# Tree attention: V's copies of the first 128 nodes move from GpSimd to VectorE, and loads and stores are reordered

## The chip, the cores and the metric

The kernel runs on one core of a Trainium2 chip. The metric is device time in microseconds (us) of one execution. The kernel before takes 140.92 us (median of three runs, 140.81 to 143.45). The profile read below spans 138.3 us from the first to the last instruction; the run that it belongs to was timed at 140.06 us, so a time contains about 2 us that the span does not.

## The reference

There are 8 batches of 12 heads, so 96 heads, each with 512 positions of 64 numbers. The positions are the nodes of a binary tree in heap order, and a node attends only to itself and to its ancestors:

```python
mask = np.zeros((seq, seq))
for i in range(seq):
    mask[i, i] = 1
    parent = i
    while parent > 0:
        parent = (parent - 1) // 2
        mask[i, parent] = 1
scores = np.einsum('bhqd,bhkd->bhqk', Q, K) * scale
scores = scores + (1 - mask) * (-1e9)
weights = np.exp(scores - np.max(scores, axis=-1, keepdims=True))
weights = weights / (np.sum(weights, axis=-1, keepdims=True) + 1e-10)
return np.einsum('bhqk,bhkd->bhqd', weights, V).astype(np.float32)
```

Q, K and V are float32 of 12.58 MB each, and so is the output.

## The kernel before, in words

**Units of work.** Heads are loaded by groups of eight (the code's `o`, here an *octet*; there are 12), computed by pairs (`i`, 48 iterations, four to an octet) and stored by groups of four (`q`, 24 stores of two iterations each). Position 4p+t of a head lies in partition p, slot t.

**Loads (lines 179 to 205).** Every load is a DMA that GpSimd issues, and each turns float32 into bfloat16 on the way, so 2 bytes are read from memory for each byte that lands. An octet takes six: K and Q (512 KB each as landed), V's partitions 64 to 127 (256 KB), V's partitions 32 to 63 straight into the value tile `vt` in two pieces (64 KB each, line 201), and V's partitions 0 to 31 (128 KB). The staging pools hold four octets. There are four value tiles.

**V's copies.** `values` needs V rows in the order of the key tiles. `spread_top` (line 207) copies V's partitions 0 to 31, the nodes under 128, into all four quarters of the value tile with four copies of 32 x 512 numbers; before the change they run on GpSimd (line 209). `spread_leaves` (line 221) and `spread_l7` (line 234) rearrange the rest on VectorE: three copies of 64 x 1024 numbers for an octet (lines 223 and 236). The first octet has forms of its own by four heads (line 245).

**One iteration.** TensorE does `scores1(i)` and `scores2(i)` (lines 292 to 329), then `values(i - 1)` (line 346), then `transpose(i + 2)` (line 259, K's part first, then Q's). ScalarE takes the exponentials of both score tiles (lines 307 and 331). VectorE does `norm(i - 1)`: a reciprocal (line 372) and a multiplication (line 375) that frees the only output tile `ob`; then `evac(i + 2)`, which copies the transposed K and Q out of PSUM (line 285) and frees the only transpose tile `kqp`; then what `spread_vector(i)` hands it. Every engine works in the order written.

**The order on GpSimd.** `pool_program` (line 394) is a list written by hand: loads of octet `o`, then `spread_top(o - 1)`, then two stores that lie `BEHIND` = 8 groups behind the loads, and so on for `o` = 2 to 11; at the end the remaining stores, with the last `spread_top` among them. In the compiled program each of GpSimd's DMAs waits for the landing of the eighth one before it, so at most eight are under way; an octet's six loads and two stores are eight. The last group of four heads is stored in pieces by the queues of SyncE and ScalarE.

**The order on VectorE.** `spread_vector(i)` (line 435) takes `divmod(i + 2, 4)`: at i = 4o - 2 the first leaf copy of octet o, at i = 4o - 1 the second one and `spread_l7`. `values` of octet o begins in iteration 4o + 1.

Of the kernel before, what the change touches and what calls it, by code (L numbers as in the profile page):

```python
# [107 lines left out]
def kernel(  # L108
# [7 lines left out]
    nc = tc.nc  # L116
# [4 lines left out]
    NQ = B * H // 4  # L121
# [57 lines left out]
    def load(kept, name, pool, src, o, h0=0, n=8, rows=(0, 128)):  # L179

        if o not in kept:
            kept[o] = pool.tile([P, 8, 4, D], bf16, name=name)
        nc.gpsimd.dma_start(  # L183
            out=kept[o][rows[0]:rows[1], h0:h0 + n, :, :].rearrange("p h t d -> p h (t d)"),
            in_=src[rows[0]:rows[1], 8 * o + h0:8 * o + h0 + n, :],
        )

    def load_k(o, h0=0, n=8):
        load(ksts, "kst", loads, Kr, o, h0, n)

    def load_q(o, h0=0, n=8):
        load(qsts, "qst", loads, Qr, o, h0, n)

    def load_v(o, *args):
        load(vsts, "vst", vloads, Vr, o, *args)

    def load_v_tiles(o):

        load_v(o, 0, 8, (64, 128))
        for half in range(2):  # L200
            nc.gpsimd.dma_start(  # L201
                out=vts[o % NV][32 * half:32 * half + 32, :, VCOL[1]:VCOL[1] + 2 * D],
                in_=Vr[32:64, 8 * o:8 * o + 8, 2 * D * half:2 * D * half + 2 * D],
            )
        load_v(o, 0, 8, (0, 32))

    def spread_top(o, h0=0, h1=8):
        for j in range(4):
            nc.gpsimd.tensor_copy(  # L209
                out=vts[o % NV][32 * j:32 * j + 32, h0:h1, VTOP:VTOP + D],  # L210
                in_=vsts[o][0:32, h0:h1, UNITS[TOP + j][1], :],
            )

    def tile_pair(o, p, h0, h1, first):

        c, step = VCOL[first], VCOL[first + 2] - VCOL[first]
        return vts[o % NV][p:p + 64, h0:h1, c:c + 2 * step].rearrange(
            "p h (t d) -> p h t d", t=2
        )[:, :, :, 0:D]

    def spread_leaves(o, upper, h0=0, h1=8):

        nc.vector.tensor_copy(  # L223
            out=tile_pair(o, 64 if upper else 0, h0, h1, upper),
            in_=vsts[o][64:128, h0:h1, upper:3 + upper:2, :],
        )
# [7 lines left out]
    def spread_l7(o):  # L234

        nc.vector.tensor_copy(  # L236
            out=tile_pair(o, 64, 0, 8, 0),
            in_=swapped(vts[o % NV][0:64, :, VCOL[3]:VCOL[3] + D], -D),
        )
# [142 lines left out]
    def store(eng, q, h0=0, n=4):  # L382
        eng.dma_start(  # L383
            out=Or[:, 4 * q + h0:4 * q + h0 + n, :],
            in_=ofs[q][:, h0:h0 + n, :, :].rearrange("p h t d -> p h (t d)"),
        )


    BEHIND = 8

    AHEAD = 3
    NO = NQ // 2

    def pool_program():

        for h0 in (0, 2):
            load_k(0, h0, 2)
            load_q(0, h0, 2)
        load_v(0, 0, 4)
        load_k(0, 4, 4)  # L400
        load_q(0, 4, 4)
        load_v(0, 4, 4)
        load_k(1, 0, 4)
        load_q(1, 0, 4)
        spread_top(0, 0, 4)
        load_v_tiles(1)
        load_k(1, 4, 4)
        load_q(1, 4, 4)
        spread_top(0, 4, 8)
        yield  # L410
        yield
        for o in range(2, NO):
            load_k(o)
            load_q(o)
            load_v_tiles(o)
            spread_top(o - 1)
            yield
            for q in (2 * o - BEHIND, 2 * o + 1 - BEHIND):
                if q >= 0:
                    store(nc.gpsimd, q)  # L420
        for q in range(NQ - BEHIND, NQ - 1):
            yield
            store(nc.gpsimd, q)
            if q == NQ - BEHIND + AHEAD:
                spread_top(NO - 1)

    def spread_first(quad, parts):

        for part in parts:
            if part < 4:  # L430
                spread_l7_natural(0, part, 4 * quad, 4 * quad + 4)
            else:
                spread_leaves(0, part - 4, 4 * quad, 4 * quad + 4)

    def spread_vector(i):

        if i == 1 or i == 2:
            spread_first(1, range(3) if i == 1 else range(3, 6))
        o, step = divmod(i + 2, 4)
        if 1 <= o < NO:  # L440
            if step == 0:
                spread_leaves(o, 0)
            elif step == 1:
                spread_leaves(o, 1)
                spread_l7(o)

    def pool_until(done, wanted):
        while done < wanted:
            next(program, None)
            done += 1  # L450
        return done

    program = pool_program()
    steps = pool_until(0, 1)
    transpose(0)
    evac(0)
    for i in range(NP + 1):
        if i < NP:
            scores1(i)
            scores2(i)  # L460
        if i == 1:
            transpose(2)
            evac(2)
            spread_first(0, range(4, 6))
        if i >= 1:
            values(i - 1)
            norm(i - 1)
        for n in (1 if i == 0 else i + 2,):
            if n < NP:
                transpose(n)  # L470
                evac(n)
        if i == 0:
            spread_first(0, range(4))
        spread_vector(i)
        if steps < NO:
            steps = pool_until(steps, min((i + 11) // 4, NO))
        else:
            steps = pool_until(steps, min(steps + 2, NO + (i - 2) // 2 - (NQ - 1 - BEHIND)))
        if i == NP - 1:
            store(nc.sync, NQ - 1, 0, 2)  # L480
# [32 lines left out]
```

The softmax here doesn't subtract the row's maximum and nothing guards it: scores larger than these inputs give would overflow.

## Time and profile before

| | before |
|---|---|
| time, median | 140.92 us |
| span of the profile | 138.3 us |
| granted TensorE clock, mean | 0.972 |
| busy: TensorE, VectorE, ScalarE, GpSimd | 107.7, 96.5, 84.3, 102.1 us |
| GpSimd's copies (line 209) | 52 copies, 31.1 us |
| first K landed, first exponential | 5.2 us, 8.05 us |
| exponential of iterations 7 and 47 starts | 30.48 us, 130.12 us |
| last multiplication of `norm` ends | 134.3 us |

The page of a profile gives busy times by engine, then the span in 40 slices of 3.46 us with the busy tenths of each engine, the share of the DMA engines and the rate at which bytes landed. The groups below it name a source line, an engine, an operation with its shapes, its count, its busy time, the mean of one in ns, and what ended the idle time before it. The waits say who sat idle until whom. The timeline lists instructions as start, duration, engine, line, operation, with the idle time ahead of it in square brackets. `L209` is line 209.

GpSimd's busy time counts the issuing of DMAs; a large one takes it 0.75 to 0.9 us. The landing rate counts bytes as they arrive in bfloat16, so a load of 197 GB/s reads 394 GB/s of memory.

### The profile page before, as it was taken

What the parts mean: (1) busy time and instruction counts of PE and PEld (TensorE: products, weight loads), DVE (VectorE), ACT (ScalarE), POOL (GpSimd) and SP (SyncE); (2) the same over time, 40 slices, a digit from 0 to 9 for tenths busy, and PEclk for the clock granted to TensorE, in tenths of its full rate; (3) what the DMA queues carried; (4) which work ended last, traced back from release to release, by engine and by line L of the source; (5) the groups of instructions that cost most, each with busy time, mean ns of one, the idle gap of its engine ahead of it and who ended that gap; (6) DMA issues with size and microseconds to landing.
All of it is one profiled execution on the core that took longest, in us unless ns stands there. A gap on an engine that the chain in (4) does not pass through costs nothing.

```text
span 138.3 us, 5482 instructions
## 1 busy us (share of the span) xinstructions
PE 107.7 (78%) x2400; PEld 78.6 (57%) x2400; DVE 96.5 (70%) x205; ACT 84.3 (61%) x98; POOL 102.1 (74%) x155
## 2 busy tenths in 40 slices
PE   0486798799879996968998995795895894997920
PEld 0243566577656774746676674574574583675610
DVE  4036688889788698759698884684784775788550
ACT  4044075768775866848686774595595486486810
POOL 6969999749599896797598399489489489489200
PEclk9999689999999999999999999999999999999985
DMA  4999999999999999999999999999999999999982
GB/s 137 155 136 189 195 192 197 198 191 198 192 198 194 335 220 195 323 227 197 295 254 196 280 272 194 257 291 198 244 303 198 229 315 202 221 366 390 364 302 92
DMA packets 44936, 32.27 MB, mean 233 GB/s; under 512 B 7280, under 2 KB 41840, under 8 KB 44912
## 3 DMA queue, kind: packets, MB, share of 16 engines
q0 software_dynamic: 44208, 30.94, 127.2%
q1 hardware_dynamic: 560, 0.85, 1.8%
q8 instruction: 18, 0.29, 0.8%
q10 hardware_dynamic: 144, 0.13, 0.3%
q14 instruction: 6, 0.05, 0.1%
HBM read 38.21 MB, written 12.58 MB: 367 GB/s over the span
## 4 chain that ended last, share of the span: by engine, by line
PE 34%; DMA 27%; DVE 16%; POOL 9%; issue 9%; ACT 1%; POOLq 0%; ACTq 0%
DMA qst<-in_Q_dram 27%; PE ob L346 15%; PE kqp L259 8%; DVE of L375 5%; PE s L296 4%; POOL vt L209 3%; DVE vt L223 3%; DVE kq L285 3%; PE s L301 3%; DVE vt L236 3%; PE s L325 3%; PE s L318 2%; DVE rec L372 2%; POOL kst L183 2%; POOL out_dram L383 1%
## 5 line engine op out<-in xcount | busy, mean ns | idle before, releaser
L307 ACT ACTIVATE e<-s 128x1024 bf16<-128x1024 f32 x48 | 49.1, 1023 | 46.8 <-PE s L301 46.1
L346 PE MATMUL ob<-vt,e 128*128 128x65 bf16 (+1 forms) x960 | 39.3, 198 | 14.3 <-POOL vt L209 7.1
L346 PEld LDWEIGHTS <-e 128*128 128x128 bf16 (+1 forms) x960 | 31.3, 103 | 20.8 <-issue 9.3
L285 DVE COPY kq<-kqp 128x1024 bf16<-128x1024 bf16 x48 | 32.8, 683 | 9.5 <-PE kqp L259 9.4
L331 ACT ACTIVATE e<-s 128x768 bf16<-128x768 f32 x48 | 38.6, 805 | 0.0
L375 DVE TENSOR_TENSOR of<-ob,rec 128x512 f32<-128x512 f32 x48 | 33.2, 692 | 1.9 <-DMA out_dram<-of 0.2
L209 POOL COPY vt<-vst 32x512 bf16<-32x512 bf16 (+1 forms) x52 | 31.1, 598 | 3.5 <-DMA vst<-in_V_dram 1.3
L372 DVE RECIPROCAL rec<-ob 128x8 f32<-128x8 f32 x48 | 9.9, 207 | 23.7 <-PE ob L346 23.2
L259 PE MATMUL kqp<-ctile,qst 128*64 128x128 bf16 x384 | 20.1, 226 | 5.3 <-DMA qst<-in_Q_dram 3.2
L259 PE MATMUL kqp<-ctile,kst 128*64 128x128 bf16 x384 | 19.7, 225 | 5.2 <-DMA kst<-in_K_dram 5.2
L183 POOL DMA_DIRECT2D qst<-in_Q_dram x15 | 12.7, 849 | 11.7 <-PE kqp L259 6.6
L383 POOL DMA_DIRECT2D out_dram<-of x23 | 17.6, 768 | 5.0 <-DVE of L375 4.7
L325 PEld LDWEIGHTS <-kq 64*128 64x128 bf16 x384 | 15.9, 97 | 7.1 <-issue 1.6
L296 PE MATMUL s<-ctile 64*128 64x512 bf16 x96 | 19.4, 400 | 0.1
L301 PE MATMUL s<-kq 64*128 64x512 bf16 x96 | 18.9, 391 | 0.5 <-DVE kq L285 0.5
L183 POOL DMA_DIRECT2D vst<-in_V_dram x24 | 16.2, 676 | 2.4 <-DMA vt<-in_V_dram 2.4
L325 PE MATMUL s<-kq 64*128 64x96 bf16 (+3 forms) x384 | 17.9, 213 | 0.1
L259 PEld LDWEIGHTS <-qst 128*64 128x64 bf16 x384 | 14.0, 114 | 5.4 <-DMA qst<-in_Q_dram 4.3
L318 PE MATMUL s<-ctile 64*128 64x384 bf16 x96 | 16.2, 334 | 0.2
L259 PEld LDWEIGHTS <-kst 128*64 128x64 bf16 x384 | 12.9, 114 | 5.4 <-DMA kst<-in_K_dram 5.2
L201 POOL DMA_DIRECT2D vt<-in_V_dram x22 | 12.7, 585 | 4.1 <-DMA qst<-in_Q_dram 2.2
L183 POOL DMA_DIRECT2D kst<-in_K_dram x15 | 13.0, 868 | 2.2 <-POOLq L497 0.8
(15 smaller groups left out, 42.3 us busy)
## 6 DMA issues: line engine op xcount, KB each, us to landing
out_dram<-of POOLq DMA_DIRECT2D x23, 512.0 KB, 8.2
kst<-in_K_dram POOLq DMA_DIRECT2D x10, 512.0 KB, 10.0
qst<-in_Q_dram POOLq DMA_DIRECT2D x10, 512.0 KB, 10.1
vst<-in_V_dram POOLq DMA_DIRECT2D x13, 256.0 KB, 10.1
vt<-in_V_dram POOLq DMA_DIRECT2D x22, 64.0 KB, 9.7
vst<-in_V_dram POOLq DMA_DIRECT2D x11, 128.0 KB, 9.7
kst<-in_K_dram POOLq DMA_DIRECT2D x3, 256.0 KB, 7.2
qst<-in_Q_dram POOLq DMA_DIRECT2D x3, 256.0 KB, 7.6
```

The source lines that it names most:

```text
L183: nc.gpsimd.dma_start(out=kept[o][rows[0]:rows[1], h0:h0 + n, :, :].rearrange("p h t d -> p h (t d)"), in_=src[rows[0]:rows[1], 8 * o + h0 ...
L209: nc.gpsimd.tensor_copy(out=vts[o % NV][32 * j:32 * j + 32, h0:h1, VTOP:VTOP + D], in_=vsts[o][0:32, h0:h1, UNITS[TOP + j][1], :],)
L259: nc.tensor.transpose(out=dst, in_=st[i // 4][:, 2 * (i % 4) + a, t, :], identity=perm)
L285: nc.vector.tensor_copy(out=kq[:, :, :, :].rearrange("p k (x y) c -> p k x (y c)", x=2), in_=src)
L296: nc.tensor.matmul(out=sp[:, a, :], lhsT=k1code[64 * a:64 * a + 64, :], rhs=q1code[64 * a:64 * a + 64, :], start=True, stop=False,)
L301: nc.tensor.matmul(out=sp[:, a, :], lhsT=keys(i, a, TOP), rhs=qTs[i][64 * a:64 * a + 64, :, :].rearrange("p t c -> p (t c)"), start=False, ...
L307: nc.scalar.activation(out=et[:, :, :, :].rearrange("p a t c -> p (a t c)"), in_=sp[:, :, :].rearrange("p a c -> p (a c)"), func=AF.Exp, s ...
L325: nc.tensor.matmul(out=sp[:, a, :, :].rearrange("p t c -> p (t c)")[:, lo:hi], lhsT=keys(i, a, TILE2[tile2]), rhs=qTs[i][64 * a:64 * a + 6 ...
L331: nc.scalar.activation(out=e2s[i % NE][:, :, :, 32:128].rearrange("p a t c -> p (a t) c"), in_=sp[:, :, :, 32:128].rearrange("p a t c -> p ...
L346: nc.tensor.matmul(out=ob[lo:hi, a, start_o:start_o + 65], lhsT=e[:, a, QPOS[t], lo:hi], rhs=vt[:, 2 * (i % 4) + a, col:col + 65], **flags,)
L375: nc.vector.tensor_tensor(out=ofs[q][:, 2 * r:2 * r + 2, :, :], in0=vals, in1=rec[:, :, :, :].to_broadcast([P, 2, 4, D]), op=ALU.mult,)
L383: eng.dma_start(out=Or[:, 4 * q + h0:4 * q + h0 + n, :], in_=ofs[q][:, h0:h0 + n, :, :].rearrange("p h t d -> p h (t d)"),)
```

## The change

`spread_top` gets the engine as an argument. For the first octet it stays on GpSimd, where it waits for its data among the first loads; for octets 1 to 11 it moves to VectorE, one iteration ahead of the two leaf copies, and the schedule of `spread_vector` moves by one iteration so that all three leaf copies of octet o now lie at i = 4o and `spread_top(o)` at i = 4o - 1. GpSimd is left with the issuing of DMAs, which no longer waits for its own copies. The first K and Q come by four heads, not by two, which takes two DMAs away from the start. Stores lie ten groups behind the loads, not eight, so that loads come earlier in the queue, and the rest of the stores follow after the last load without anything between them.

```diff
-    def spread_top(o, h0=0, h1=8):
+    def spread_top(eng, o, h0=0, h1=8):
         for j in range(4):
-            nc.gpsimd.tensor_copy(
+            eng.tensor_copy(
                 out=vts[o % NV][32 * j:32 * j + 32, h0:h1, VTOP:VTOP + D],
                 in_=vsts[o][0:32, h0:h1, UNITS[TOP + j][1], :],
             )
...
-    BEHIND = 8
-
-    AHEAD = 3
+    BEHIND = 10
     NO = NQ // 2
 
     def pool_program():
 
-        for h0 in (0, 2):
-            load_k(0, h0, 2)
-            load_q(0, h0, 2)
+        load_k(0, 0, 4)
+        load_q(0, 0, 4)
         load_v(0, 0, 4)
...
-        spread_top(0, 0, 4)
+        spread_top(nc.gpsimd, 0, 0, 4)
         load_v_tiles(1)
         load_k(1, 4, 4)
         load_q(1, 4, 4)
-        spread_top(0, 4, 8)
+        spread_top(nc.gpsimd, 0, 4, 8)
         yield
         yield
         for o in range(2, NO):
             load_k(o)
             load_q(o)
             load_v_tiles(o)
-            spread_top(o - 1)
             yield
...
         for q in range(NQ - BEHIND, NQ - 1):
             yield
             store(nc.gpsimd, q)
-            if q == NQ - BEHIND + AHEAD:
-                spread_top(NO - 1)
...
-        o, step = divmod(i + 2, 4)
+        o, step = divmod(i + 1, 4)
         if 1 <= o < NO:
             if step == 0:
+                spread_top(nc.vector, o)
+            elif step == 1:
                 spread_leaves(o, 0)
-            elif step == 1:
                 spread_leaves(o, 1)
                 spread_l7(o)
```

## The prediction

> **What bounds the kernel now.** I read the slices of the page first, then the rate of landing in short windows, the waits, and last the timeline of VectorE.
>
> ```profile
> DMA  4999999999999999999999999999999999999982
> GB/s 137 155 136 189 195 192 197 198 191 198 192 198 194 335 220 195 323 227 197 295 254 196 280 272 194 257 291 198 244 303 198 229 315 202 221 366 390 364 302 92
> HBM read 38.21 MB, written 12.58 MB: 367 GB/s over the span
> ```
>
> The DMA engines are at nine tenths or more from the second slice to the 38th. Where only loads run, 192 to 198 GB/s land; where only stores run, 366 to 390. A landed byte of a load costs two read bytes, so both are one rate. The windows say it more exactly (columns: window, length, busy time of PE, PEld, DVE, ACT and POOL with counts, clock, DMA share, GB/s):
>
> ```profile
> 2.00:10.00 8.00, 4.41 (x48) 2.52 (x48) 1.24 (x6) 1.95 (x4) 6.73 (x10) 1.00 1.13 170
> 50.00:54.00 4.00, 2.95 (x77) 2.16 (x78) 3.83 (x8) 2.72 (x4) 3.75 (x6) 1.00 1.46 198
> 122.00:126.00 4.00, 3.73 (x91) 2.74 (x88) 3.54 (x8) 3.31 (x5) 3.71 (x6) 1.00 1.06 397
> 134.00:138.00 4.00, 0.00 (x0) 0.00 (x0) 0.25 (x1) 0.00 (x0) 0.00 (x0) 0.51 0.35 121
> ```
>
> 2 x 198 = 396 and 397 GB/s: this is memory traffic at its limit. 50.79 MB at 393 GB/s take 129.2 us of the 138.3 us span. What remains to be won is the slow start (2 to 10 us), and the end, where after 126 us stores wait for compute. So the transfers are one bound. Compute is the other, nearly level with it:
>
> ```profile
> DVE rec L372 <- PE ob L346: 23.2, 33, 1.7
> PE ob L346 <- POOL vt L209: 7.1, 5, 1.7
> PE kqp L259 <- DMA qst<-in_Q_dram: 3.2, 6, 0.9
> ```
>
> In the first half the exponential of an iteration starts every 2.07 us where nothing disturbs, and an octet (iterations 4 to 28 on average) takes (80.89 - 23.28)/6 = 9.6 us. From iteration 28 on it takes 10.6 us, which is the transfers' pace: (3.146 MB read + 1.049 MB written)/0.393 = 10.7 us. There TensorE waits 1.5 to 1.7 us an octet for GpSimd's copies and 0.3 to 0.7 for Q. Removing the first wait alone would only lengthen the second. Finally VectorE around a pair of spread copies in iterations 6 and 7:
>
> ```profile
> 31.00 0.45 DVE L223 COPY vt<-vst 64x1024 bf16<-64x1024 bf16 x1
> 32.35 0.68 DVE L285 COPY kq<-kqp 128x1024 bf16<-128x1024 bf16 x1
> 33.06 0.43 DVE L223 COPY vt<-vst 64x1024 bf16<-64x1024 bf16 x1
> 33.52 0.72 DVE L236 COPY vt<-vt 64x1024 bf16<-64x1024 bf16 x1
> 34.27 0.21 DVE L372 RECIPROCAL rec<-ob 128x8 f32<-128x8 f32 x1
> 34.52 0.69 DVE L375 TENSOR_TENSOR of<-ob,rec 128x512 f32<-128x512 f32 x1
> 35.35 0.78 PE L346 MATMUL ob<-vt,e 128*128 128x65 bf16 x20 [0.49 <-DVE of L375]
> 36.17 0.21 DVE L372 RECIPROCAL rec<-ob 128x8 f32<-128x8 f32 x1 [0.37 <-PE ob L346]
> ```
>
> VectorE's own work in an iteration is 0.25 + 0.61 + 0.71 = 1.57 us from start to start, 0.5 less than the 2.07. The single copy at 31.00 disappears in that. The two at 33.06 hold the next reciprocal until 34.27, that is 1.21 us, and TensorE then loses 0.49: the slack is about 0.7 us an iteration, and the iteration after a delay has 0.17 less (0.37 idle instead of 0.54).
>
> **What the Trainium skill says.** "SBUF — State Buffer", Who interferes with whom: VectorE copies in a two-port mode and GpSimd share a port pair by an exclusive lock, GpSimd's descriptor writing included. The trace agrees in part: line 236 takes 0.42 us in its shortest instances and 0.72 to 0.75 beside a GpSimd copy or store issue. "VectorE: DVE Perf Modes", the perf-mode tier table: a bfloat16 copy in SBUF moves four numbers a cycle. Line 223 with 1024 numbers takes 0.42 undisturbed, with 512 numbers 0.30; 0.12 for 512 agrees with 512/4 cycles at 0.96 GHz = 0.13. "DMA: Bandwidth & Descriptors", Issuing engines are not separate DMA queues: all transfers share the same 16 engines; the flat 393 GB/s here is what they give.
>
> **The change part by part.** *GpSimd's copies.* 44 copies of 635 ns, 28 us, leave GpSimd. It isn't the bound, so what goes is TensorE's 7.1 us of waits, and only as far as the transfers allow.
>
> *The copies on VectorE.* The nearest row is line 245, 32 x 512:
>
> ```profile
> L245 DVE COPY vt<-vst x8: 283/377/558, 10.5 to 20.4; 32x512 bf16<-32x512 bf16 x8
> L236 DVE COPY vt<-vt x11: 420/719/753, 24.7 to 124.6; 64x1024 bf16<-64x1024 bf16 x11
> ```
>
> I take 0.32 us from start to start (0.28 and the gap); four are 1.28 us, with 0.39 (its mean) as upper end 1.56. After i = 4o - 1 this delays TensorE by 1.28 - 0.69 = 0.59 us. One iteration later the three leaf copies follow at once: 0.46 each undisturbed, 1.38; delay 1.38 - 0.52 = 0.86. Both sum to 1.45 us an octet where the schedule before lost about 0.5. Upper end: 1.56 and 1.75 give 0.87 + 1.23 = 2.10. Behind the copies on VectorE queue `norm` and `evac`, for which TensorE waits with `values` and `transpose`; this is the added wait.
>
> *Other stalls.* In iterations 4 to 28 the octet's 9.6 us exceed 4 x 2.07 + 0.5 by 0.8 us: TensorE idle with no releaser ("issue": 1.00, 1.05, 1.17 us at 41, 53 and 60 us) and small ones. They do not appear after 80 us, where TensorE waits for other things. Part of them will coincide with VectorE's delays, and GpSimd's issues (about 6 us an octet) will still block some copies: I take 0.5 together, 0 to 0.8 as bounds. An octet of compute then takes 8.27 + 1.45 + 0.5 = 10.2 us; lower end 9.7, upper 10.6.
>
> *First loads.* Two issues of 0.73 us go. The second half of the first octet's Q, issued at 5.71 us and landing at 12.83, starts the part of the chain that sets iteration 2; it is issued 1.4 us earlier, and I let it land 1 us earlier (0 to 1.4; the transfers ahead are the same bytes). The very first scores come later, since K of four heads must land, but they have 4 us to spare before 12.83. Iteration 3 loses 1.67 us of contended copies and gets 1.28. I take iteration 7 at 29.2 us instead of 30.48.
>
> *Stores further behind.* 12 instead of 14 stores come before the last loads: 2 x 0.524 MB/0.393 = 2.7 us; with the start (0.5) the last Q lands at 117.0 instead of 120.2 us. No store waits in GpSimd's list for `norm` until the tail. Eleven stores, 14.7 us, follow, beside about 17 us of computing.
>
> *Sum.* Iterations 7 to 47 are ten octets: 29.2 + 10 x 10.2 - 0.3 (the last iteration has no transposes) = 130.9 us, against 130.12. The transfers would allow less (below), so VectorE's pace decides. The tail of 8.2 us stays: the last stores are short and wait for `norm`. +0.8 on 140.9 gives 141.7 us.
>
> **The rivals.** *Transfers stay the bound.* If the copies run undisturbed and other stalls hide, 9.7 us an octet would end iteration 47 at 126; then the last Q decides: iteration 43 started 1.1 us after it, at 118.1 now, and 4 x 2.07 - 0.3 + 1.45 later iteration 47, at 127.5: 2.6 us earlier, 138.3 us. For it: GpSimd's copies, the worst disturbers, are gone, and after 80 us line 236 took 0.42. Against it: VectorE gets two loaded iterations in a row. *VectorE becomes the bound outright.* With the upper ends, 8.27 + 2.10 + 0.2 = 10.57: 29.2 + 105.7 - 0.3 = 134.6, 4.5 later, 145.4 us, slower. For it: in the first 80 us line 236 took 0.72 beside store issues with no GpSimd copy near, and GpSimd will do nothing else but issue. Against it: line 223 took 0.42 beside many issues of V.
>
> **How the numbers follow.** Forecast 141.7 with 0.48; transfers the bound, 138.3, 0.27; VectorE outright, 145.4, 0.25. The 2% bounds lie at 138.1 and 143.7. Half of the second case, uncertain by 1 us, falls under: 0.12 faster. Most of the third falls above, 0.22. The range from 138.0 to 145.0 leaves out the fastest and slowest tails of the two rivals.
>
> **What would show it.** In the profile after: four copies of line 209 on VectorE at about 0.28 us, 1.3 us of them an octet; TensorE's wait for GpSimd gone, in its place waits for line 375 after each pair of loaded iterations, some 1.4 us an octet; no more Q waits in the second half; an octet at 10.2 us; last Q landed near 117. If Q waits persist and octets after 80 us stay at 10.6, the transfers bound. If line 209 takes 0.4 or octets pass 10.5, the second rival holds. I would be wrong in another way if memory traffic fell under 393 GB/s, or if GpSimd's descriptor writing starved behind VectorE's copies.

## The result, and the profile after

The changed kernel takes 152.64 us (median of four runs, 151.01 to 159.15) against 140.87 us for the kernel before (now four runs): a ratio of 1.081 [1.069, 1.093]. One run of each, 159.15 and 143.45 us, is well above the others of its kernel and is left out of the ratio. The change makes the kernel slower by 11.8 us, well outside the predicted range. Its profile spans 150.3 us against 138.3, and the mean granted clock of TensorE is 0.942 against 0.972.

First the page of the changed kernel: clock, DMA share and landing rate by slices (here of 3.76 us), the memory total, and the first line of the chain that ended last.

```profile
PEclk9999999999999999999599999999999697799595
DMA  4999999999999999999999999999999999243053
GB/s 128 160 191 196 191 198 201 190 201 188 199 191 198 195 339 201 204 334 196 225 310 199 253 283 197 284 251 197 302 235 197 339 407 364 79 140 123 21 174 108
HBM read 38.21 MB, written 12.58 MB: 338 GB/s over the span
...
PE 45%; DVE 41%; issue 7%; DMA 4%; POOL 1%; POOLq 0%
```

The transfers are not slower. The bulk of their work is done after 34 of 40 slices; the last six show the DMA engines at 0 to 5 tenths. In the chain DMA has 4%; in that of the kernel before it had 27%, and VectorE 16% instead of 41%. The windows of the changed kernel say the same for the stretches shown before (same columns: window, length, busy time of PE, PEld, DVE, ACT and POOL with counts, clock, DMA share, GB/s):

```profile
2.00:10.00 8.00, 2.30 (x22) 1.11 (x24) 0.98 (x5) 0.22 (x2) 5.85 (x10) 1.00 1.20 187
50.00:54.00 4.00, 4.00 (x103) 3.00 (x99) 2.85 (x7) 2.79 (x4) 1.78 (x3) 1.00 1.45 238
122.00:126.00 4.00, 2.23 (x53) 1.57 (x50) 3.83 (x11) 3.06 (x4) 0.75 (x1) 1.00 1.01 385
134.00:138.00 4.00, 2.22 (x53) 1.57 (x50) 3.83 (x11) 3.05 (x4) 0.75 (x1) 1.00 0.22 74
```

From 2 to 10 us more lands (187 instead of 170 GB/s). From 122 us stores alone run, still at 385. But TensorE, which was busy for 3.73 of 4.00 us there before, is busy for 2.23, beside a VectorE that is busy for 3.83. The last Q landed at 117.2 us instead of 120.2; the last exponential of the first kind (line 307, iteration 47) started at 143.04 instead of 130.12. What TensorE waited for (columns: total us, times, longest):

```profile
DVE rec L372 <- PE ob L346: 28.3, 36, 1.7
...
PE ob L346 <- DVE vt L236: 19.2, 11, 1.9
...
PE ob L346 <- DVE of L375: 4.8, 12, 1.1
```

The wait for GpSimd (7.1 us) is gone, and no Q wait remains after the start. In their place stands a wait of `values` for line 236, the last of the three leaf copies: 11 times, once for each octet that has these copies, about 1.75 us each. VectorE's timeline around one octet shows how it comes about (start, duration, engine, line, operation, idle time ahead):

```profile
109.94 1.16 DVE L209 COPY vt<-vst 32x512 bf16<-32x512 bf16 x4
...
111.14 0.21 DVE L372 RECIPROCAL rec<-ob 128x8 f32<-128x8 f32 x1
111.38 0.69 DVE L375 TENSOR_TENSOR of<-ob,rec 128x512 f32<-128x512 f32 x1
...
111.99 0.68 DVE L285 COPY kq<-kqp 128x1024 bf16<-128x1024 bf16 x1
112.13 0.30 PE L346 MATMUL ob<-vt,e 128*128 128x65 bf16 x4 [0.27 <-DVE of L375]
...
112.68 1.07 DVE L223 COPY vt<-vst 64x1024 bf16<-64x1024 bf16 x2
113.79 0.42 DVE L236 COPY vt<-vt 64x1024 bf16<-64x1024 bf16 x1
114.26 0.65 PE L346 MATMUL ob<-vt,e 128*128 128x65 bf16 x16 [1.84 <-DVE vt L236]
```

The four top copies delay `norm`, and TensorE loses 0.27 us. Then it begins `values` of the octet's first pair at 112.13. Its first four products read only the top tile; the fifth reads what the leaf copies write. These were put into the iteration directly ahead, begin after `evac` at 112.68 and end at 114.21. TensorE stands for 1.84 us. Together 2.1 us are lost in this octet, and an iteration that takes 2.07 us elsewhere takes about 4.2 (from 36.19 to 40.38 us in an earlier octet).

The copies themselves are as cheap as forecast (line: count, duration min/median/max in ns, first and last start):

```profile
L209 DVE COPY vt<-vst x44: 269/283/425, 24.1 to 134.9; 32x512 bf16<-32x512 bf16 x44
...
L236 DVE COPY vt<-vt x11: 420/421/422, 27.8 to 137.9; 64x1024 bf16<-64x1024 bf16 x11
```

Octets, from the start of line 307 in iteration 7 on:

| | iteration 7 | ten octets, us | iteration 47 |
|---|---|---|---|
| before | 30.5 | 8.8, 10.0, 9.5, 10.5, 9.2, 11.0, 10.6, 10.5, 10.6, 8.8 | 130.1 |
| after | 32.1 | 10.4, 10.5, 10.6, **12.2**, 10.4, 10.8, 10.6, **12.1**, **12.0**, **11.5** | 143.0 |

Six octets take 10.53 us on average (10.39 to 10.78). Four take 11.5 to 12.2, and these hold something else. Windows of 2 us of the changed kernel around the first of them (columns as above):

```profile
68.00:70.00 2.00, 0.30 (x4) 0.21 (x5) 1.94 (x5) 1.36 (x2) 0.89 (x2) 1.00 1.47 196
70.00:72.00 2.00, 1.57 (x36) 1.15 (x37) 1.22 (x4) 0.00 (x0) 0.70 (x1) 0.86 1.45 198
72.00:74.00 2.00, 2.00 (x30) 1.34 (x28) 0.65 (x2) 1.40 (x2) 0.22 (x2) 0.50 1.54 192
```

After the wait TensorE's clock is granted at one half for 3.4 us; from 72 to 74 us it is busy throughout and gets through 30 matmuls, where it gets through 52 in two busy microseconds at full clock (42 to 44 us). This happened four times between 71 and 143 us.

So the 12.0 us by which the span grew are: 1.6 up to iteration 7, of which 1.1 belong to the iteration with the first of the eleven waits; 10 x 10.53 - 99.6 = 5.7 for the octets at full clock; 5.7 for the four at half clock (47.8 - 4 x 10.53); and 0.9 back in the tail (7.3 instead of 8.2 us).

### The profile page after: what moved, and what is told of

The parts are those of the page before. It is cut to its first block, busy times and chain, and to the rows that moved or that the text cites. A ratio compares the mean times of both kernels' runs of the same rounds, so it can differ in the third digit from the quotient of the medians.

```text
span 150.3 us, 5460 instructions
## 1 busy us (share of the span) xinstructions
PE 111.8 (74%) x2400; PEld 81.4 (54%) x2400; DVE 104.8 (70%) x249; ACT 84.3 (56%) x98; POOL 73.1 (49%) x109
## 3 DMA queue, kind: packets, MB, share of 16 engines
q0 software_dynamic: 44176, 30.94, 117.0%
## 4 chain that ended last, share of the span: by engine, by line
PE 45%; DVE 41%; issue 7%; DMA 4%; POOL 1%; POOLq 0%
PE ob L346 18%; DVE kq L285 11%; PE kqp L259 9%; DVE vt L223 8%; DVE vt L209 8%; DVE of L375 7%; PE s L296 6%; PE s L301 5%; DMA qst<-in_Q_dram 4%; PE s L325 4%; DVE rec L372 4%; PE s L318 3%; DVE vt L236 3%; POOL kst L183 1%; DVE vt L245 0%
## 5 line engine op out<-in xcount | busy, mean ns | idle before, releaser
L346 PE MATMUL ob<-vt,e 128*128 128x65 bf16 (+1 forms) x960 | 41.8, 201 | 26.1 <-DVE vt L236 19.2
L346 PEld LDWEIGHTS <-e 128*128 128x128 bf16 (+1 forms) x960 | 32.4, 105 | 34.2 <-issue 19.0
L383 POOL DMA_DIRECT2D out_dram<-of x23 | 17.7, 769 | 27.2 <-DVE of L375 19.7
L325 PEld LDWEIGHTS <-kq 64*128 64x128 bf16 x384 | 16.8, 100 | 7.1 <-issue 2.8
L296 PE MATMUL s<-ctile 64*128 64x512 bf16 x96 | 20.4, 413 | 0.2 <-issue 0.2
L301 PE MATMUL s<-kq 64*128 64x512 bf16 x96 | 20.0, 408 | 0.5 <-DVE kq L285 0.5
L183 POOL DMA_DIRECT2D kst<-in_K_dram x14 | 12.2, 869 | 14.0 <-PE ob L346 9.7
L325 PE MATMUL s<-kq 64*128 64x160 bf16 (+3 forms) x384 | 18.6, 217 | 0.0
L183 POOL DMA_DIRECT2D qst<-in_Q_dram x14 | 12.0, 860 | 12.1 <-PE s L301 6.0
L318 PE MATMUL s<-ctile 64*128 64x384 bf16 x96 | 17.2, 350 | 0.0
L259 PEld LDWEIGHTS <-kst 128*64 128x64 bf16 x384 | 13.2, 116 | 6.9 <-DMA kst<-in_K_dram 6.7
L209 DVE COPY vt<-vst 32x512 bf16<-32x512 bf16 x44 | 12.7, 288 | 0.5
## 6 DMA issues: line engine op xcount, KB each, us to landing
out_dram<-of POOLq DMA_DIRECT2D x23, 512.0 KB, 10.2
qst<-in_Q_dram POOLq DMA_DIRECT2D x10, 512.0 KB, 10.3
vst<-in_V_dram POOLq DMA_DIRECT2D x13, 256.0 KB, 10.2
```

What stands on the lines that cost most here:

```text
L183: nc.gpsimd.dma_start(out=kept[o][rows[0]:rows[1], h0:h0 + n, :, :].rearrange("p h t d -> p h (t d)"), in_=src[rows[0]:rows[1], 8 * o + h0 ...
L209: eng.tensor_copy(out=vts[o % NV][32 * j:32 * j + 32, h0:h1, VTOP:VTOP + D], in_=vsts[o][0:32, h0:h1, UNITS[TOP + j][1], :],)
L259: nc.tensor.transpose(out=dst, in_=st[i // 4][:, 2 * (i % 4) + a, t, :], identity=perm)
L296: nc.tensor.matmul(out=sp[:, a, :], lhsT=k1code[64 * a:64 * a + 64, :], rhs=q1code[64 * a:64 * a + 64, :], start=True, stop=False,)
L301: nc.tensor.matmul(out=sp[:, a, :], lhsT=keys(i, a, TOP), rhs=qTs[i][64 * a:64 * a + 64, :, :].rearrange("p t c -> p (t c)"), start=False, ...
L318: nc.tensor.matmul(out=sp[:, a, :, 32:128], lhsT=k2code[64 * a:64 * a + 64, :], rhs=q2code[64 * a:64 * a + 64, :].rearrange("p (t c) -> p ...
```

## The experiments

Theory 1, *place*: what costs is that `values(4o)` needs the leaf copies in the iteration after the one that got them. Theory 2, *crowding*: what costs is the amount of copying that VectorE gets in two successive iterations, wherever it lies. A third question is what the half clock adds. All ratios are to the kernel before, with 95% intervals.

**One iteration earlier.** The changed kernel with all seven copies moved by one iteration: top copies at i = 4o - 2, leaf copies at 4o - 1. The amounts and their crowding stay.

```diff
-        o, step = divmod(i + 1, 4)
+        o, step = divmod(i + 2, 4)
```

> The changed kernel with every VectorE spread of octets 1 to 11 one iteration earlier (top copies at i = 4o-2, the three leaf copies at i = 4o-1); same copies, same count. Theory 1 (values of octet o stands in the very next iteration after i = 4o and waits for the leaf copies themselves, 1.84 us an octet): the wait of line 346 for line 236 goes to zero, an octet falls from 10.5 to about 9.7 us, time 139 to 143. Theory 2 (VectorE has too much work in two consecutive iterations, wherever they lie): the wait moves to line 375, an octet stays at 10.4, time 150 to 153.

139.42 us, 0.992 [0.989, 0.996]: 13.2 us less than the changed kernel, and faster than the kernel before as well. The chain of this kernel, then its waits, then two neighbouring `values` of its timeline:

```profile
DVE 40%; PE 26%; DMA 17%; issue 8%; POOL 4%; ACT 1%; POOLq 0%; ACTq 0%
```

```profile
PE ob L346 <- DVE of L375: 15.4, 23, 1.1
```

```profile
34.99 0.79 PE L346 MATMUL ob<-vt,e 128*128 128x65 bf16 x20 [0.46 <-DVE of L375]
37.90 0.79 PE L346 MATMUL ob<-vt,e 128*128 128x65 bf16 x20 [0.78 <-DVE of L375]
```

There is no wait for line 236. VectorE still holds TensorE, but only through `norm`, twice an octet: for 0.46 and 0.78 us in the octet shown. The octets take 9.66 us on average (9.44 to 9.94) and none has the half clock. With the leaf copies one iteration early, the prediction's 8.27 + 1.45 = 9.72 holds nearly exactly; its 0.5 for other stalls did not come.

**The top copies back on GpSimd.** Leaf copies at their old places as well; loads, stores and start as in the changed kernel.

```diff
             load_v_tiles(o)
+            spread_top(nc.gpsimd, o - 1)
...
-        o, step = divmod(i + 1, 4)
+        o, step = divmod(i + 2, 4)
             if step == 0:
-                spread_top(nc.vector, o)
-            elif step == 1:
                 spread_leaves(o, 0)
+            elif step == 1:
```

> The changed kernel with spread_top back on GpSimd and the leaf copies where they were before; ten groups behind and the first loads by four heads stay. Theory 1 and theory 2 both: the loss goes, 138 to 142; under theory 3 (the order of loads and stores or the first loads cost the time) it stays over 148.

139.52 us, 0.993 [0.990, 0.996], level with the run above. Moving the 44 copies from GpSimd to VectorE is worth nothing measurable, either way, once the leaf copies lie early.

**No top copies.** The changed kernel without the top copies of octets 1 to 11; this leaves that part of V out, and a memset takes its place. The leaf copies stay late.

```diff
             if step == 0:
-                spread_top(nc.vector, o)
+                pass
```

> The changed kernel without the top copies of octets 1 to 11 (the copies of nodes under 128 are left out, their columns are zero); the leaf copies stay at i = 4o. Theory 1: the wait for line 236 stays at about 1.7 us an octet, because it is made by the leaf copies' place; octet 10.0 us, 145 to 149. Theory 2: with 1.2 us of VectorE's work an octet gone the loss nearly goes, 139 to 142.

142.61 us, 1.014 [1.010, 1.017]. Its waits (lines shifted by two):

```profile
PE ob L348 <- DVE vt L238: 16.6, 11, 1.9
```

With 1.2 us of VectorE work less in each octet the wait for the leaf copies is still there, 11 times and 1.5 us on average. Place alone makes it. But the time is under the 145 to 149 that were expected, and 142.6 is not 152.6. The two profiles differ by 10.9 us: 5.3 are shorter octets (10.00 us on average, 9.8 to 10.3, against 10.53), since the 0.27 through `norm` is gone and the wait is 0.24 shorter; 5.7 are the half clock, of which this profile has none after 20 us.

**Leaf copies late in the kernel before.** The other way round: the kernel before, with nothing changed but that all three leaf copies come at i = 4o.

```diff
-        o, step = divmod(i + 2, 4)
-        if 1 <= o < NO:
-            if step == 0:
-                spread_leaves(o, 0)
-            elif step == 1:
-                spread_leaves(o, 1)
-                spread_l7(o)
+        o, step = divmod(i + 1, 4)
+        if 1 <= o < NO and step == 1:
+            spread_leaves(o, 0)
+            spread_leaves(o, 1)
+            spread_l7(o)
```

> The kernel before with only one edit: the three leaf copies of an octet all at i = 4o. GpSimd keeps the top copies. Theory 1: waits for line 236 of about 1.7 us an octet appear, 144 to 149. Theory 2 (amount of work): within 1% of before, since VectorE does the same work as before.

142.99 us, 1.018 [1.010, 1.026]. Its waits:

```profile
PE ob L346 <- DVE vt L236: 17.5, 11, 2.1
```

The same wait appears, with no top copy on VectorE. It costs 2.6 us, less than expected, and not 11 x 1.6 = 17.5, since it takes the place of other waits: from 30 to 134 us TensorE waited 15.6 us in the kernel before (7.1 for GpSimd, 2.8 for `norm`, 2.1 for Q, 3.6 with no releaser) and waits 16.0 us here, all for line 236.

**Top copies apart from late leaf copies.** Top copies at 4o - 2, leaf copies at 4o: an iteration without copies between them.

```diff
-        o, step = divmod(i + 1, 4)
+        o, step = divmod(i + 2, 4)
             if step == 0:
                 spread_top(nc.vector, o)
-            elif step == 1:
+            elif step == 2:
```

> The changed kernel with the top copies one iteration earlier (i = 4o-2) and the leaf copies left at i = 4o, so one free iteration lies between them. Theory 1: the leaf copies still stand right ahead of values; wait for line 236 of 1.4 to 1.6 us and 0.5 us more for the top copies, octet 10.2 to 10.4 us, 145 to 151. Theory 2 (crowding of two loaded iterations): with them apart the octet falls to 9.7 us, 139 to 142.

148.72 us, 1.057 [1.052, 1.063]. Its waits:

```profile
PE ob L346 <- DVE vt L236: 16.5, 11, 1.7
```

Taking the crowding away while the place stays late leaves the wait and most of the loss. The undisturbed octets take 10.07 to 10.69 us, about as in the changed kernel; one octet has the half clock. Crowding is not the main cause.

So the two halves of the change cost little apart. The late leaf copies cost 2.6 us in the kernel before, and about 3 us without top copies (142.6 against 139.5 in the run above with the leaf copies at their old places); the top copies on VectorE cost nothing where the leaf copies are early. Together they cost 13 us. This fits the sums above: the waits are then more than those whose place they take, and the half clock comes on top.

**All seven copies at once, in time.** All at i = 4o - 1: crowded as much as can be, at the place that was good in the first experiment.

```diff
                 spread_top(nc.vector, o)
-            elif step == 1:
                 spread_leaves(o, 0)
```

> The changed kernel with all seven copies of an octet (2.6 us) in one iteration, i = 4o-1, so that values of the octet stands one full iteration behind them. Theory 1 (a copy costs TensorE what exceeds the slack of about 0.7 us through norm, but its whole length where values of the same octet comes next): 8.27 + (2.6 - 0.7) = 10.2 us an octet, wait on line 375, none on line 236. Theory 2 (crowding on VectorE is what costs): as bad as the change or worse, 10.5 us or more, 150 us.

147.51 us, 1.050 [1.046, 1.055]. Its waits:

```profile
PE ob L346 <- DVE of L375: 20.4, 13, 2.3
```

The wait for the leaf copies is gone, but `norm` now stands behind 2.7 us of copies and TensorE waits up to 2.3 us for it. Undisturbed octets take about 10.1 us, 0.45 more than with the same copies over two iterations. The profile shows the half clock in five stretches, one of them before iteration 7, so it has a part in this time. Theory 2 is thus true in a narrower form: what exceeds an iteration's slack costs, and one long piece of idle TensorE can cost twice, when the half clock follows.

**The wait filled with work.** The changed kernel, with 14 matmuls of 64x240 added that nobody uses, in `values(4o)` between the fourth product and the fifth, where TensorE would stand.

```diff
                 product(e1, a, t, VTOP, start=t == 0, stop=False)
+            if a == 0 and i % 4 == 0 and i >= 4:
+                for _ in range(14):
+                    nc.tensor.matmul(
+                        out=ob[:, 0, 264:504], lhsT=k1code[0:64, :], rhs=q1code[0:64, 0:240],
+                        start=False, stop=False, skip_group_check=True,
+                    )
```

> The changed kernel plus 14 idle matmuls (64x240 into unused columns of the output tile, about 0.1 us each) in values of the first pair of octets 1 to 11, behind the four products with the top nodes, just where TensorE waits 1.84 us for line 236. No result depends on them. Theory A (about half of the loss is TensorE at half clock, granted after windows in which it sat idle): with the wait filled the half-clock stretches in mid-kernel go, mean clock 0.97 or more, time 144 to 148, while the octets keep 10.4 us. Theory B (the clock falls for another reason, and the waits alone cost the time): clock stays near 0.94, time 151 to 155.

149.62 us, 1.056 [1.050, 1.062], so 3.0 us less than the changed kernel although it does more; the two intervals do not meet. It is a smaller gain than expected (144 to 148). Its clock by slices, and the place in its timeline:

```profile
PEclk9999997799999999999999999999999999999995
```

```profile
48.79 0.30 PE L346 MATMUL ob<-vt,e 128*128 128x65 bf16 x4 [0.27 <-DVE of L381]
49.02 1.60 PE L358 MATMUL ob<-ctile 64*128 64x240 bf16 x14
50.72 0.65 PE L346 MATMUL ob<-vt,e 128*128 128x65 bf16 x16
```

The added matmuls fill the wait and no more. The half clock at 23.9 to 27.9 us comes before the first of them; from then to the end no slice falls below full clock, and the octets take 10.3 to 11.0 us. The mean clock of the four runs is 0.970 to 0.980, against 0.930 to 0.971 in the changed kernel. So in mid-kernel the half clock is a consequence of TensorE's standing. What it costs is less sure: 3.0 us between the medians, 5.7 us by the octets of the profiled run; and the runs of the changed kernel follow their clock only loosely (151.01 us at 0.971, 152.90 at 0.962, 152.38 at 0.942).

**The order of the stores alone.** The kernel before, with one number changed.

```diff
-    BEHIND = 8
+    BEHIND = 10
```

> The kernel before with stores ten groups behind the loads, alone. If the order of loads and stores moves the end: last Q 2.7 us earlier, 138 to 140 (up to 2.5 us less). If compute sets the end anyway: no change within 0.3%.

140.74 us, 1.002 [1.000, 1.004]: no gain. Nor do the loads come earlier: in its profile (of a run of 142.96 us) the last Q is issued at 110.0 us, against 110.2 in the kernel before.

**The first loads alone.** The kernel before, with the first K and Q by four heads.

```diff
-        for h0 in (0, 2):
-            load_k(0, h0, 2)
-            load_q(0, h0, 2)
+        load_k(0, 0, 4)
+        load_q(0, 0, 4)
```

> The kernel before with the first K and Q by four heads, alone. As predicted blind: iteration 2 one microsecond earlier, time 0.5 to 1 us less. Rival, seen in the profile after: the first scores come 2 us later and make up for it, time the same within 0.3%, or up to 1 us more.

139.80 us, 0.995 [0.992, 0.998]. The first exponential comes 2.0 us later (10.0 instead of 8.05 us) and iteration 7 1.3 us later (31.8), yet the whole is 0.7 us faster. The time came as expected, but not by the expected way: iteration 2 starts at 17.7 us, not a microsecond before 17.5. It fits the kernel before being held by its transfers: with two loads fewer at the start 183 instead of 170 GB/s land from 2 to 10 us, and compute made up the delay later. That this is the reason was not tested apart.

**The store order with the good schedule.** The first experiment with eight groups behind instead of ten.

```diff
-    BEHIND = 10
+    BEHIND = 8
```

> The version with every spread one iteration earlier (139.4 us), with stores eight groups behind the loads again. If the order of loads and stores matters once VectorE's copies no longer hold TensorE: the last loads land 2.7 us later and the end follows in part, 140.5 to 142. If not: 139 to 140, within 0.5% of the version with ten.

140.66 us, 1.003 [1.000, 1.006]. Here the two groups matter: 0.992 against 1.003. Iteration 47 starts at 131.5 us instead of 128.8, and the last three octets take 10.5 to 10.6 us, the pace of the transfers. The last Q is issued at 109.7 us instead of 106.9: here the two groups bring the last loads forward by 2.7 us, which they did not do alone in the kernel before.

**Copies spread over four iterations.** The changed kernel with two top copies at 4o - 4, two at 4o - 3, the first leaf copy at 4o - 2, the other two at 4o - 1 (octet 1 has its four top copies at i = 2); the octet's small V load is issued ahead of K so that the top copies have their data in time.

```diff
-        o, step = divmod(i + 1, 4)
+        o, step = divmod(i + 4, 4)
...
+            if step < 2 and o > 1:
+                spread_top(nc.vector, o, 0, 8, (2 * step, 2 * step + 1))
+            elif step == 2:
                 spread_leaves(o, 0)
+            elif step == 3:
                 spread_leaves(o, 1)
                 spread_l7(o)
```

> The changed kernel with VectorE's copies spread evenly: two top copies each at i = 4o-4 and 4o-3, the first leaf copy at 4o-2, the other two at 4o-1; V's first 32 partitions are loaded ahead of K from octet 2 on, so that they are there. Every iteration's extra work is then near its slack of 0.6 us: octets of 8.6 to 9.0 us where loads are there, then the transfers bound, with the last Q at about 117: 136.5 to 138.5 us. If a VectorE iteration waits for V's landing instead, a wait of line 210 for vst appears and the time is over 139.5.

139.78 us, 0.995 [0.992, 0.998]: not better than the first experiment, and above the 136.5 to 138.5 that were expected. The first five octets take 9.0 to 9.7 us, but three of the later ones 10.2 to 10.5, and TensorE waits for Q again, as two lines of the timeline show. Iteration 47 starts 2.0 us earlier than in the first experiment (126.8 us), and the end does not follow: the span is 137.6 against 137.0 us.

```profile
107.00 0.41 PE L260 MATMUL kqp<-ctile,qst 128*64 128x128 bf16 x8 [1.49 <-DMA qst<-in_Q_dram]
...
117.46 0.41 PE L260 MATMUL kqp<-ctile,qst 128*64 128x128 bf16 x8 [1.51 <-DMA qst<-in_Q_dram]
```

**The same without top copies.** Left out as in the other run without them: octets 1 to 11.

```diff
...
-        if o == 1 and step == 2:
-            spread_top(nc.vector, o)
         if 1 <= o < NO:
             if step < 2 and o > 1:
-                spread_top(nc.vector, o, 0, 8, (2 * step, 2 * step + 1))
+                pass
```

> The evenly spread version without the top copies of octets 1 to 11 (left out; their columns are zero). If the transfers bound the even version, taking 1.2 us an octet from VectorE gains nothing: 139 to 140. If VectorE still bounds it: 136 to 138.

139.17 us, 0.994 [0.990, 0.997]. Taking 1.2 us of VectorE work from each octet gains next to nothing (0.994 against 0.995): VectorE does not bound this version. With the waits for Q this points to the transfers, and to about 139 us as what this plan of loads and stores gives.

## Why the prediction was wrong

**The step that failed.** "One iteration later the three leaf copies follow at once ... delay 1.38 - 0.52 = 0.86", with the statement that "behind the copies on VectorE queue `norm` and `evac`, for which TensorE waits with `values` and `transpose`; this is the added wait". The working let the copies reach TensorE only through what queues behind them, and set the slack of VectorE against them. It never asked who reads what the copies write. The front matter had the answer: `values` of octet o begins in iteration 4o + 1, the very next one after i = 4o. The copies come last in their iteration on VectorE, behind `evac`. Ahead of the reader in the next iteration are only the scores, which TensorE does while VectorE is still at `norm`, and four products; there is no slack to set against the copies. Worked out with the prediction's own durations, for the octet shown above: when `values(4o)` starts, VectorE has just begun `evac` (0.68 us, say 0.6 left) and then has the three copies (1.38); the fifth product can run 2.0 us after the start, and the four before it take 0.3, so TensorE loses 1.7 us. Measured there: 1.84 (1.75 on average). With the 0.27 that the top copies cost through `norm` it is 2.0 to 2.1 us an octet, not 1.45. The kernel with the copies one iteration earlier, in which the neglected reader is far away, gives 9.66 us for the octet where the working's 8.27 + 1.45 says 9.72. The slack arithmetic was good for copies that reach TensorE through `norm`; it was applied to a schedule in which another edge comes first. Leaving the place as it was and taking away the top copies (1.014), or the place alone in the kernel before (1.018), shows the same wait.

**"+ 0.5 other stalls"** was too much: 10.53 - 8.27 - 2.1 leaves about 0.2 us. So the octet at full clock is off by only 0.33 us (10.53 against 10.2), 3.3 us over ten, because two wrong terms partly cancel.

**The half clock** is in no step. It adds 5.7 us in the profiled run, about 3 us between medians. Iteration 47 was forecast at 130.9 us and started at 143.0: 2.9 us of that are the later iteration 7, 3.3 the octets at full clock, 5.7 the half clock. The second rival forecast 145.4 us, and octets past 10.5 were to speak for it. That rival had the right size for an octet (10.57) but for a wrong reason: it wanted copies slowed by GpSimd's issues, and line 236 took 0.42 us in all 11 instances.

**The start, "iteration 7 at 29.2 instead of 30.48".** Measured 32.1. "The very first scores come later ..., but they have 4 us to spare" failed. The K of four heads lands at 6.7 us instead of 5.2, the first exponential starts at 10.2 instead of 8.05, and iteration 2 starts at 17.46 against 17.48: the earlier Q did not set it any more, and the microsecond forecast there did not come. The rest of the lateness arises after iteration 3, which still starts 0.4 us earlier than before. Two waits of `values` make most of it:

```profile
20.59 0.28 PE L346 MATMUL ob<-vt,e 128*128 128x65 bf16 x4 [0.74 <-DVE of L375]
28.25 0.65 PE L346 MATMUL ob<-vt,e 128*128 128x65 bf16 x16 [1.62 <-DVE vt L236]
```

The first is for `norm`, which stands behind copies of the first octet on VectorE; before, there was no wait at this place. Iteration 3 takes 4.16 us instead of 3.33, where the forecast had it shrink. The second is the first of the eleven waits of the failed step, and iteration 5 takes 4.18 instead of 3.06. The first loads alone, in the kernel before, also bring iteration 7 late (31.8 us), but by another sum: there iteration 4 takes 3.52 us at half clock.

**What was right.** Line 209 at 0.28 us on VectorE; line 236 at its undisturbed 0.42; the wait for GpSimd gone; no Q waits in the second half; the last Q at 117.2 us (117.0 forecast); memory traffic as dense as before where anything was to be moved. The claim that GpSimd's copies cost TensorE only "as far as the transfers allow" holds too: with them back on GpSimd the time is the same as with them on VectorE at the good place (0.993 and 0.992).

**When the half clock comes** can be read from the same trace. "TensorE: Matmul & The Clock Gate", Part 1, has the clock fall to half after an idle window of about 3.4 us, in windows that run freely, and asks for no idle gaps over about 3.4 us. The windows agree: the four stretches begin at 71.44, 115.81, 126.05 and 139.70 us, so 13, 3 and 4 times 3.413 us apart, and each lasts one such window. The rule on gaps is not enough: no single wait of the matmuls in mid-kernel reached 2 us, yet the clock fell; the measurement decides. What the four have in common shows when the trace is cut on that grid (columns as above). The first four lines are the windows directly ahead of the four stretches, the last one is the least busy of all others between 13 and 143 us:

```profile
68.03:71.44 3.41, 1.31 (x36) 1.09 (x36) 2.56 (x7) 1.33 (x2) 1.00 (x3) 1.00 1.46 197
112.40:115.81 3.41, 1.57 (x39) 1.17 (x39) 2.57 (x7) 0.93 (x2) 1.40 (x2) 1.00 1.47 196
122.64:126.05 3.41, 1.59 (x33) 0.99 (x29) 3.27 (x8) 2.42 (x3) 0.75 (x1) 1.00 1.01 382
136.29:139.70 3.41, 1.55 (x40) 1.19 (x41) 2.57 (x6) 1.10 (x2) 0.75 (x1) 1.00 0.44 154
47.55:50.96 3.41, 1.84 (x46) 1.39 (x45) 2.57 (x7) 0.86 (x3) 1.74 (x3) 1.00 1.46 196
```

The half clock followed where TensorE was busy for 1.31 to 1.59 of 3.41 us, and nowhere where it was busy for 1.84 or more. Other kernels on their own grids agree, from 30 us to the last exponential: with all copies at once it followed windows of 1.42 to 1.56 us and not those of 1.65 and more; with the top copies apart it followed one of 1.75; without top copies no window is under 1.79, and with the wait filled none under 2.56, and there is no half clock. The line therefore lies near half of a window: a wait of 1.8 us that falls whole into one window leaves about 1.6 us of it, just on that line, and a wait that is split between two windows leaves more in each. So nearly equal waits did it four times of eleven; it may also be why runs of one kernel differ.

**What stays open** is the exact condition: at the start and the end of runs the half clock also followed windows with 1.75 to 2.04 us busy, so the busy time of TensorE is not all that counts.

## What to carry to other kernels

When work moves to another place in an engine's order, follow two edges from it: what queues behind it, against which the slack counts, and the first reader of what it writes, against which nothing counts but the time between. An engine with free time on average still makes its neighbour stand if the reader comes in the next iteration; one iteration of lead was worth 13 us of 152 here, the half clock included. And once TensorE stands for almost 2 us at a time, read the granted clock as well as the wait, since the wait may be paid for a second time.

## What the hardware did unexpectedly

- TensorE's clock was granted at one half for 3.4 us at a time, four times in the changed kernel, each time after a window of 3.41 us in which TensorE was busy for 1.31 to 1.59 us, though no single wait in it reached 2 us; 14 useless matmuls of 1.6 us in each wait removed it, and the kernel became 3.0 us faster.
- Beside an issue of GpSimd a VectorE copy may grow, or the issue, or neither. In the kernel of the first experiment line 236 took 0.68 us at 94.1 us, where a K issue of the usual 0.89 us had begun 0.44 us earlier; at 75.3 us it took 0.42, and the Q issue that had begun 0.19 us earlier took 1.09; at 104.2 us it took 0.42, and a K issue begun 0.09 us later its usual 0.89. That agrees only in part with the exclusive lock of "SBUF — State Buffer", Who interferes with whom: the loss was 0.2 to 0.3 us or none, and at 75.3 us the one that came first had it. The changed kernel's steady 0.42 us isn't the merit of cheaper issues: at ten of the eleven instances GpSimd was issuing nothing.
- In the kernel before, the first loads by four heads start compute 2 us later and end the kernel 0.7 us earlier: 183 instead of 170 GB/s land between 2 and 10 us.
